# Attention over 128 half heads on one core: three planner constants, a planner that may mix two chains, K's second copy in two halves, fewer self-waits

## The chip, the cores and the metric

One core of a Trainium2 chip (trn2). The metric is the device time of one execution in microseconds (us), lower is better. Ratios are the mean time of one kernel's fast runs over the mean of the other's fast runs of the same rounds, so not quite the ratio of the medians that are quoted.

## The reference

```python
q (8, 8, 1024, 64), k and v (8, 2, 1024, 64), float32, values about 0.1
for each of 2 key/value heads, for its 4 query heads:
    scores = q @ k.T / 8
    attn = exp(scores - max);  attn /= attn.sum() + 1e-8
    out = attn @ v
```

The kernel leaves out the maximum (scores are small) and divides by the sum at the end; the sum comes from a column of ones beside v.

## The kernel before: the parts that matter

In the lines of the profile `aps` is a PSUM buffer with two scores for ScalarE, `dps` a bank with one score for VectorE, `ops` a bank of outputs (PSUM is the memory in which TensorE's results lie here, a bank one piece of it); `p_ring` and `pd` hold finished exponentials, `z` and `y` what a chain has in between, `kset` K.

There are 128 jobs (8 batches, 8 heads, even and odd query rows), each of 8 cells of 128 keys by 512 queries, 1024 cells in all. A cell needs a score matmul (`qk`) on TensorE, an exponential, and an output product (`pv`, four matmuls of 65 columns). Two roads lead through the exponential:

- road A, ScalarE: two cells at once (a *pair* of scores) in one of two PSUM buffers, one `exp` of 128x1024;
- road D, VectorE with GpSimd: a *conversion* (`p1`) of one cell into 16-bit integers, then for each ten cells a *chain* of four steps that corrects the bits: `and`, `line` (on GpSimd), `prod`, `add`.

`norm` is the normalisation of a finished job on VectorE (a reciprocal and a multiplication). Which cell takes which road, and in which order each engine works, is decided by a greedy planner in the kernel, which keeps a clock for every engine and always takes the operation that it believes can start first:

```python
QK, PV, P1, NORM = 0.216, 0.1225, 0.603, 0.555
EXP = (0.05, 0.4268)
FOUR, TWO, POOL_ONE = (0.20, 0.133), (0.16, 0.27), (0.25, 0.43)   # fixed, per cell: and / prod, add / line
... AHEAD = 0.04                                                  # lead of the scores for ScalarE
FIRST_TURN = 3.3                                                  # when the odd side's K is there
...
while normed < nj:
    ...                                        # road A: one more score of a pair
            best = min(best or (INF,), (t - AHEAD, 1, "qk", 0, t))
    ...                                        # road D: one more score for VectorE
            best = min(best or (INF,), (t, 2, "qk", 1, t))
    ...                                        # pv, norm, p1, and the first chain in the queue
```

The engines run the operations in this order, whatever time they really take. In an exp:

```python
if n >= P_TILES and n % OBSERVE == 0:          # P_TILES = 28 output tiles in a ring, OBSERVE = 8
    seen = exp_ins[n - P_TILES + OBSERVE - 1]
    tc.add_manual_dep(act.ins, seen.name, SYNC, reason="ring")      # self-wait: ScalarE for ScalarE
```

At the start, the even side's K lies in partitions 0 to 63 and is copied to partitions 64 to 127 for the odd side:

```python
nc.scalar.copy(out=qT[(0, 0)][:, : HALF // 2], in_=tq[0][:, : HALF // 2])
turn_k(1, slice(0, NHC), 0)
last_score[0] = keep_warm(4)
put_k(0, 1, slice(0, NHC), 0)
nc.gpsimd.dma_start(out=ksets[0][hi, 0, 1, :], in_=ksets[0][lo, 0, 0, :])
```

The softmax here doesn't subtract the row's maximum and nothing guards it: scores larger than these inputs give would overflow.

## Time and profile before

| | before |
|---|---|
| time | 386.97 us, median of 3 (386.77 to 387.01) |
| span of the traced execution | 384.92 us |
| exps, conversions | 406, 212 |
| end of the fourth exp | 10.82 us |
| distance between the ends of later exps | 0.917 us |
| last exp ends, then to the end | 379.33, 5.59 us |

The lines behind this table are in the prediction below. How to read it: ScalarE's exps form one row without holes from the fourth to the last, so the time is the start, plus the number of exps times 0.917 us, plus every lateness of an exp, plus what follows the last. I number exps from 0 ("the fourth" is number 3). *Late* means: the end of an exp lies more than 0.917 us behind the end of the one before; the surpluses of 5 ns or more are added up, good to about 0.01 us. In before, from the fifth exp on, they come to 0.01 us.

### The profile page before, as it was taken

How to read it: one execution, taken by the hardware profiler on the slowest of the kernel's cores; microseconds unless marked ns; L12 is line 12 of the kernel's file. 1: busy time of each engine (PE TensorE's matmuls, PEld its weight loads, DVE VectorE, ACT ScalarE, POOL GpSimd, SP SyncE). 2: the span in 40 equal slices, each digit the busy share in tenths (PEclk: the TensorE clock that was granted, in tenths of full speed). 3: DMA queues.
4: the chain of work that ended last, by engine and by line, in shares of the span. 5: the costliest groups of instructions: out<-in, count | busy, mean ns of one | idle time of the engine just before them, and what ended most of it. 6: DMA issues, size and time to landing. Idle time of an engine off the chain costs nothing.

```text
span 384.9 us, 12057 instructions
## 1 busy us (share of the span) xinstructions
PE 368.1 (96%) x5172; PEld 234.5 (61%) x5172; DVE 350.1 (91%) x544; ACT 375.1 (97%) x411; POOL 165.3 (43%) x147
## 2 busy tenths in 40 slices
PE   8879999999999999999999999999999999999985
PEld 6425565656666666666666565666566566666654
DVE  4879999999999999999999999999999999999692
ACT  5999999999999999999999999999999999999994
POOL 5394571716246171625535252535445261531410
PEclk9999999999999999999999999999999999999998
DMA  8888979597859769595865949486584756621213
GB/s 137 152 130 141 141 138 173 113 129 148 128 111 134 132 109 141 123 138 85 151 123 126 125 90 169 74 150 113 119 143 109 111 100 113 109 70 29 71 43 83
DMA packets 102422, 45.49 MB, mean 118 GB/s; under 512 B 63776, under 2 KB 100896, under 8 KB 101120
## 3 DMA queue, kind: packets, MB, share of 16 engines
q1 hardware_dynamic: 82096, 31.21, 37.5%
q0 software_dynamic: 19728, 13.25, 29.8%
q8 instruction: 40, 0.66, 0.8%
q10 hardware_dynamic: 544, 0.26, 0.2%
q14 instruction: 14, 0.11, 0.1%
HBM read 25.17 MB, written 27.00 MB: 136 GB/s over the span
## 4 chain that ended last, share of the span: by engine, by line
ACT 94%; PE 2%; DMA 1%; issue 1%; DVE 0%; SPq 0%; POOLq 0%
ACT p_ring L463 94%; PE ops L522 1%; PE aps L452 1%; DMA fk<-in_k_dram 1%; DMA kset<-kset 1%; SPq L389 0%; DVE ost L538 0%; ACT hk L411 0%; DVE kset L382 0%; DVE qT L427 0%; PE aps L373 0%; DVE rec L535 0%; PE ops L419 0%; PE ops L400 0%; POOLq L433 0%
## 5 line engine op out<-in xcount | busy, mean ns | idle before, releaser
L463 ACT ACTIVATE p_ring<-aps 128x1024 bf16<-128x1024 f32 x406 | 372.4, 1100 | 1.2 <-PE aps L452 1.2
L452 PE MATMUL aps<-qT,kset 128*128 128x512 bf16 x812 | 240.6, 378 | 11.4 <-ACT p_ring L463 8.8
L522 PEld LDWEIGHTS <-p_ring 128*128 128x128 bf16 x3248 | 137.5, 97 | 60.4 <-ACT p_ring L463 0.2
L522 PE MATMUL ops<-vset,p_ring 128*128 128x65 bf16 x3248 | 150.8, 194 | 0.1
L477 DVE TENSOR_SCALAR pd<-dps 128x512 uint16<-128x512 f32 x212 | 138.0, 682 | 13.2 <-PE dps L452 12.3
L500 POOL TENSOR_SCALAR y<-z 128x5120 f16<-128x5120 uint16 (+1 forms) x22 | 94.6, 4301 | 82.7 <-DVE rec L535 45.0
L452 PEld LDWEIGHTS <-kset 128*128 128x128 bf16 x1024 | 82.6, 97 | 58.8 <-issue 26.7
L314 POOL DMA_DIRECT2D scr_q<-in_q_dram x63 | 34.7, 551 | 99.0 <-PE aps L452 47.6
L452 PE MATMUL dps<-qT,kset 128*128 128x512 bf16 x212 | 73.4, 378 | 0.0
L511 DVE TENSOR_TENSOR pd<-pd,y 128x5120 uint16<-128x5120 uint16 (+1 forms) x22 | 59.8, 2719 | 0.1
L509 DVE TENSOR_TENSOR y<-z,y 128x5120 f16<-128x5120 uint16 (+1 forms) x22 | 59.8, 2718 | 0.0
L538 DVE TENSOR_TENSOR ost<-ops,rec 128x256 f32<-128x256 f32 x128 | 54.3, 424 | 4.4
L522 PEld LDWEIGHTS <-pd 128*128 128x128 bf16 x848 | 41.3, 98 | 25.6 <-DVE pd L511 3.6
L522 PE MATMUL ops<-vset,pd 128*128 128x65 bf16 x848 | 48.4, 194 | 0.0
L496 DVE TENSOR_SCALAR z<-pd 128x5120 uint16<-128x5120 uint16 (+1 forms) x22 | 31.7, 1443 | 0.6
L535 DVE RECIPROCAL rec<-ops 128x4 f32<-128x4 f32 x128 | 22.5, 176 | 9.8 <-PE ops L522 8.8
L347 POOL DMA_DIRECT2D vset<-in_v_dram x32 | 24.9, 782 | 0.0
L314 POOL DMA_DIRECT2D scr_k<-in_k_dram x15 | 7.8, 521 | 24.1 <-PE aps L452 16.7
L400 PE MATMUL ops<-blank 128*128 128x128 bf16 x40 | 4.4, 286 | 1.1 <-DVE blank L279 1.1
L400 PEld LDWEIGHTS <-blank 128*128 128x128 bf16 x40 | 3.8, 135 | 1.1 <-DVE blank L279 1.1
L354 POOL DMA_DIRECT2D kset<-kset x6 | 3.2, 537 | 0.0
L411 ACT ACT_TABLE_LOAD x1 | 1.3, 1283 | 1.8 <-issue 1.8
(23 smaller groups left out, 8.7 us busy)
## 6 DMA issues: line engine op xcount, KB each, us to landing
out_dram<-ost SPq DMA_DIRECT2D x63, 256.0 KB, 2.9
scr_q<-in_q_dram POOLq DMA_DIRECT2D x63, 128.0 KB, 3.6
kset<-kT SPq DMA_DIRECT2D x60, 64.0 KB, 3.1
vset<-in_v_dram POOLq DMA_DIRECT2D x32, 64.0 KB, 4.0
scr_k<-in_k_dram POOLq DMA_DIRECT2D x15, 128.0 KB, 3.2
qT<-scr_q SPq DMA_TRANSPOSE x63, 4.0
kset<-kset POOLq DMA_DIRECT2D x7, 128.0 KB, 4.0
fq<-in_q_dram ACTq DMA_DIRECT2D x2, 128.0 KB, 3.2
```

The lines of the kernel that those rows point to most:

```text
L314: dma = nc.gpsimd.dma_start(out=scr.rearrange("(p f) -> p f", f=1024), in_=src.rearrange("(p s) d -> p (s d)", s=1024 // D),)
L347: nc.gpsimd.dma_start(out=vsets[b % 2][:, g, two * NHC : (two + 1) * NHC, 0:D], in_=v[b, g].rearrange("(c p two) d -> two p c d", p=128, t ...
L452: last_score[0] = nc.tensor.matmul(dst, lhsT=ksets[b % 2][:, h // HPG, side, c * 128 : (c + 1) * 128], rhs=qT[(b, h)], start=True, stop=Tr ...
L463: act = nc.scalar.activation(out=pt[:, 0:m], in_=psum.pop(("A", n))[:, 0:m], func=AF.Exp, scale=scale)
L477: nc.vector.tensor_scalar(out=groups[g][:, slot], in0=psum.pop(cell), scalar1=bits_scale, scalar2=bits_bias, op0=ALU.mult, op1=ALU.add,)
L496: eng.tensor_scalar(out=z, in0=pd, scalar1=0x7F, scalar2=None, op0=ALU.bitwise_and)
L500: eng.tensor_scalar(out=y, in0=z, scalar1=CURVE_A / 128.0, scalar2=CURVE_B, op0=ALU.mult, op1=ALU.add,)
L509: eng.tensor_tensor(out=y, in0=z, in1=y, op=ALU.mult)
L511: eng.tensor_tensor(out=pd, in0=pd, in1=y, op=ALU.add)
L522: nc.tensor.matmul(ops_of[s][:, qs, :], lhsT=p_of[cell][:, qs * 128 : (qs + 1) * 128], rhs=vsets[b % 2][:, h // HPG, c, :], start=opens an ...
L535: nc.vector.reciprocal(out=rec, in_=o[:, :, D])
L538: nc.vector.tensor_tensor(out=stage[(b, h)][:, :, side, :], in0=o[:, :, 0:D], in1=rec.unsqueeze(2).to_broadcast([128, NQS, D]), op=ALU.mult,)
```

## The change

The intent: let the planner mix the steps of two chains, with a model of the SBUF port that VectorE and GpSimd share; give it smaller fixed costs of the chain's steps and no lead for ScalarE's scores; bring half of K's second copy earlier; drop most self-waits.

```diff
-    FOUR, TWO, POOL_ONE = (0.20, 0.133), (0.16, 0.27), (0.25, 0.43)
+    FOUR, TWO, POOL_ONE = (0.09, 0.133), (0.05, 0.27), (0.25, 0.43)
-    ... AHEAD, FIRST_PV = 28, 5, 16, 2, 6, 6, 0.04, 2.0
+    ... AHEAD, FIRST_PV = 28, 5, 16, 2, 6, 6, 0.0, 2.0
-    FIRST_TURN, FIRST_LOAD, EACH_LOAD = 3.3, 4.5, 4.2
+    FIRST_TURN, FIRST_LOAD, EACH_LOAD = 2.4, 4.5, 4.2
...
+        for i, (at, _, _, step) in enumerate(chainq):
+            if CHAIN[step] in ON_POOL:
+                at = max(at, pool, two_end)
+            else:
+                at = max(at, dve, pool)
+            best = min(best or (INF,), (at, 2 + i, "chain", i))
...
-    OBSERVE = 8
+    OBSERVE = 26
-        if n >= P_TILES and n % OBSERVE == 0:
+        if n >= P_TILES and (n - P_TILES) % OBSERVE == 0:
...
+        nc.scalar.dma_start(
+            out=ksets[0][hi, 0, 1, :HALF], in_=ksets[0][lo, 0, 0, :HALF]
+        )
         turn_k(1, slice(0, NHC), 0)
         last_score[0] = keep_warm(4)
         put_k(0, 1, slice(0, NHC), 0)
-        nc.gpsimd.dma_start(out=ksets[0][hi, 0, 1, :], in_=ksets[0][lo, 0, 0, :])
+        nc.gpsimd.dma_start(
+            out=ksets[0][hi, 0, 1, HALF:], in_=ksets[0][lo, 0, 0, HALF:]
+        )
```

Cut: two constants that switch nothing on (their values are 0), the bookkeeping of the two new clocks (`pool`, `two_end`), and a test for empty chain parts.

## The prediction

> **What bounds the kernel now.** I read the page first (busy shares, chain by line, groups), then the waits, then the chain in order of time at the start and at the end, then the timelines of ScalarE and TensorE in those stretches.
>
> ```profile
> PE 368.1 (96%) x5172; PEld 234.5 (61%) x5172; DVE 350.1 (91%) x544; ACT 375.1 (97%) x411; POOL 165.3 (43%) x147
> ...
> ACT 94%; PE 2%; DMA 1%; issue 1%; DVE 0%; SPq 0%; POOLq 0%
> ...
> L463 ACT ACTIVATE p_ring<-aps 128x1024 bf16<-128x1024 f32 x406 | 372.4, 1100 | 1.2 <-PE aps L452 1.2
> L477 DVE TENSOR_SCALAR pd<-dps 128x512 uint16<-128x512 f32 x212 | 138.0, 682 | 13.2 <-PE dps L452 12.3
> ```
>
> ScalarE's exps are the path: 406 of them, 372.4 us busy, that is 0.917 us each although one lasts 1100 ns (neighbours overlap), and only 1.2 us of idle before them in the whole run. The other score cells (212 of 1024; an exp covers two cells) go through VectorE: one conversion each (L477), and for every ten cells a chain of four steps, and and prod and add on VectorE, line on GpSimd. VectorE's 13.2 us of idle before conversions is its slack.
>
> The chain in order of time, then the timelines of ScalarE and of TensorE at the start, show where the path is not ScalarE:
>
> ```profile
> 6.63 2.48 DMA kset<-kset
> 9.15 0.62 PE aps L452 x2
> ```
> ```profile
> 6.47 2.85 ACT L463 ACTIVATE p_ring<-aps 128x1024 bf16<-128x1024 f32 x3 [0.68 <-PE aps L452]
> 9.80 23.94 ACT L463 ACTIVATE p_ring<-aps 128x1024 bf16<-128x1024 f32 x26 [0.47 <-PE aps L452]
> ```
> ```profile
> 9.15 1.04 PE L452 MATMUL aps<-qT,kset 128*128 128x512 bf16 x4 [0.27 <-DMA kset<-kset]
> ```
>
> Columns of a timeline row: start, duration, then the work. Three exps run from 6.47, ending at 9.32; the fourth starts at 9.80, because its scores wait for the second copy of K (SBUF to SBUF, issued by GpSimd at 6.63, landed at 9.11). A free-standing exp takes 1.02 us from start to end, a following one ends 0.917 after the last, so the fourth ends at 10.82 where 10.24 was possible: the wait costs 0.58 us.
>
> The end, from the chain in order of time:
>
> ```profile
> 366.34 6.59 ACT p_ring L463 x7
> 372.92 0.04 issue
> 372.96 0.59 PE aps L452 x2
> ...
> 377.62 0.52 PE aps L452 x2
> 378.14 2.60 PE ops L522 x84
> ```
>
> The last exp ends at 379.33 in the timeline, but TensorE works until 380.74: after the last score it still has 84 output matmuls, 21 cells of 4, back to back (2.60 / 21 = 0.124 us a cell). So the last 1.4 us, and the normalisation behind it (0.66) and the store, follow a TensorE backlog, not the exp.
>
> **What the Trainium skill says.** "ScalarE: Activation LUTs", section "What ACT_TABLE_LOAD costs": with immediate scale and bias an ACTIVATE takes 186 ns + 0.833 ns per element, and back-to-back ones overlap by about 93 ns. For 1024 elements that is 1039 ns alone and 946 ns in a row; the trace has 1020 and 917. The measured figures decide; both say that the period is ScalarE's own, not a wait for scores. "SBUF — State Buffer", section "Who interferes with whom": a VectorE instruction with two SBUF inputs, or in a 2-port mode, and a GpSimd instruction that reads SBUF hold the shared port by turns, the later one blocks fully. The trace of before cannot test it: no and, prod or add lies beside a line, and the full lines take 4.45 to 4.48 us whatever conversions and normalisations lie beside. "DMA: Bandwidth & Descriptors", section "Latency and other measured facts": first byte about 0.6 us from a hardware-generated queue (ScalarE's, SyncE's) and 1 us from GpSimd's. I use only the direction; the GpSimd copy at hand took 2.48 us from issue to landing, ScalarE's two loads from HBM 3.1 and 3.4.
>
> **The change part by part.** The kernel's order comes from a planner inside it, so I compared the built programs' instruction orders.
>
> 1. *The new model.* Despite the intent no two chains mix: in both orders each and, line, prod, add is over before the next chain's and. What changes is the split. After has 404 exps and 216 conversions (before 406 and 212): the lower fixed costs of the chain steps let VectorE take four cells more, and the last chain has six cells, not two. On the path: 2 exps less x 0.917 = **-1.83 us**.
>  Can VectorE carry it? After places a chain about every 18 exps, 18 x 0.917 = 16.5 us. From the distances between ends in the trace, for ten cells: 10 conversions x 0.60 + 5.75 normalisations x 0.55 (0.09 + 0.46) + and 1.45 + prod 2.73 + add 2.73 = 16.1 us. It fits with 0.4 us to spare, 97% busy; before had a chain every 17 us or so. What is lost: prod now stands straight behind the earliest end of line, where before about 0.5 us lay between, so each late GpSimd start (before: 3 of 22 lines started 0.4 to 1.1 us after their and, behind DMA issues) now holds VectorE, and may hold TensorE at a conversion bank. I put **+0.2 us** on it, a guess from three such starts of which half is absorbed.
>
> 2. *Lead of score matmuls from 0.04 to 0.* TensorE may now put an output or a VectorE score in front of an exp's scores. The exps were fed with only 0.47 us of idle after the start, and each such swap is at most one score matmul, 0.216 us; most is hidden by the second PSUM buffer. **0**.
>
> 3. *K's second copy.* Its even half leaves on ScalarE's queue, where it waits only for a VectorE copy done at 4.76 and ScalarE's own copy done at 5.52, so issue at about 5.6, and not at 6.63 behind the odd half (L382 ends at 6.02). With the 2.5 to 3.1 us seen from issue to landing it lands at 8.1 to 8.7. The fourth exp's scores are free to run only when the second exp's PSUM buffer is (ends 8.40, so about 8.55), behind one more score for VectorE: at landing up to 8.35 nothing of the 0.58 us remains, at 8.7 some 0.35. The issue takes about 0.5 us of ScalarE's queue (its earlier two: 0.48 and 0.53), to 6.1, before the first exp at 6.47. The odd half is still on GpSimd, needed only from the fifth exp. **-0.45 us**, of 0.58 at most.
>
> 4. *Self-waits.* 51 exps carry a wait for an earlier exp before, 15 after. The chain shows an "issue" of about 0.04 us at each; were that real, 36 x 0.045 = 1.6 us would come back. But the 26 exps from 9.80 to 33.74 hold one such wait and run at (23.94 - 1.02) / 25 = 0.917; the 360 from 36.37 to 366.34, each eighth with one, at 329.97 / 360 = 0.917. A waiting exp starts later and ends when it would have: **0**.
>
> 5. *The end.* In the new order 13 cells of output follow the last score, not 21: 8 x 0.124 = 1.0 us less backlog. But the last exp then bounds too: it ends about 1.19 us after the last score (379.33 - 378.14), and two cells follow, 0.16 + 0.25, so 1.6 us, the same as 13 x 0.124. From 2.60 to 1.6: **-1.0 us**. In before TensorE stood idle for about 0.33 us before each of three score pairs from 369 on, with the outputs waiting for the last full chain; in after's order these outputs come earlier.
>
> Sum: -1.83 + 0.2 - 0.45 - 1.0 = -3.1 us, from 386.97 to **383.9 us** (0.992).
>
> **The rivals.**
> - *VectorE becomes the bound.* For it: 97% by my sum, and prod without slack behind line. If each of some 20 chains held up the exps by 0.15 us, +3 us: 386.9, no gain. Against: before's VectorE was idle about 21 us between 12 and 372 us by its gaps, and the additional work is 4 x 0.6 + 4 cells of chain (0.13 + 0.27 + 0.27) = 5 us.
> - *The self-waits do cost what the chain shows.* Then 1.6 us more, 382.3. Against it: point 4.
> - *The copy on ScalarE's queue delays the first exp,* or lands no sooner than GpSimd's. Then 0 to +0.4 instead of -0.45: about 384.5. For it: ScalarE's earlier DMAs took longer to land than GpSimd's copy, though from HBM.
> - *The tail's order does not hold on the chip*: the outputs of the last six-cell chain are late and the backlog stays 2.6 us: 384.9.
>
> **Range and chances.** Sure are the two exps; the others make the range: 382.7 if the self-waits pay in part and the start gains all of its 0.58, 385.8 if VectorE's stalls take 2 us. Executions of one kernel spread by 0.1% here. Faster by over 2% needs 379.2, 4.7 us beyond the sum, and no wait of that size is left; slower by over 2% needs 7.7 us of new ScalarE idle in a plan of the same kind. Chances 0.01, 0.97, 0.02.
>
> **What would show each step.** 404 exps at 0.917 each, with under 1 us of idle in total (step 1 and 2; idle before exps in the middle of the run, released by scores, means VectorE bounds). VectorE's idle before conversions falls from 13 us to under 9, and a row of waits of VectorE for line appears. The fourth exp starts at 9.2 to 9.4, the first at 6.47 as before (step 3); a first exp after 6.6 refutes it. Exps without self-wait at 0.917 confirm step 4, at 0.90 refute it. The last output run of the chain is x52, about 1.6 us, and the exp or TensorE end together (step 5). The prediction fails if exps show idle in the middle of the run, or if their period changes.

## The result, and the profile after

385.77 us, median of 4 (385.70 to 385.81), against 386.99 of before; ratio 0.9968, interval 0.9951 to 0.9986. The gain is 1.2 us where 3.1 were predicted; the time lies at the upper end of the predicted range (385.8).

From the page of the changed kernel: busy shares, the chain by engine, and two groups (after the bar: busy us, mean ns of one; then idle before, and what ended it).

```profile
PE 365.6 (95%) x5172; PEld 233.6 (61%) x5172; DVE 353.8 (92%) x548; ACT 374.6 (98%) x409; POOL 174.4 (45%) x147
...
ACT 86%; PE 10%; DVE 2%; issue 1%
...
L477 ACT ACTIVATE p_ring<-aps 128x1024 bf16<-128x1024 f32 x404 | 371.8, 1067 | 1.4 <-PE aps L466 1.2
L491 DVE TENSOR_SCALAR pd<-dps 128x512 uint16<-128x512 f32 x216 | 138.6, 683 | 7.0 <-PE dps L466 6.7
```

404 exps and 216 conversions, as read from the order. The idle time before exps is 1.4 us, no more than the 1.2 of before, so by the idle column the exps are fed as well as ever. That column misleads here. Two exps overlap by up to 0.18 us on ScalarE, so one that comes up to that much late leaves no hole. Its lateness shows in two other places of the same line: busy divided by count is 371.8 / 404 = 0.9203 (before 372.4 / 406 = 0.9172), and the mean of one fell from 1100 to 1067 ns, because a late exp spends less time overlapped with its forerunner. 404 x 0.0031 = 1.25 us is most of what is missing. The chain says it too: 10% of it now runs through TensorE, where it was 2%.

The start. First four transposes and the first scores on TensorE's timeline, before, then after:

```profile
5.18 0.39 PE L373 MATMUL dps<-ident,hk 128*128 128x128 bf16 x4
5.84 1.02 PE L452 MATMUL aps<-qT,kset 128*128 128x512 bf16 x4
```
```profile
5.73 0.63 PE L382 MATMUL dps<-ident,hk 128*128 128x128 bf16 x4
```
```profile
5.94 0.56 ACTq L439 DMA_DIRECT2D kset<-kset  x1
7.40 23.94 ACT L477 ACTIVATE p_ring<-aps 128x1024 bf16<-128x1024 f32 x26 [1.23 <-PE aps L466]
```

The same four transposes took 0.63 instead of 0.39 us (314 against 219 ns each): TensorE was still at its slow clock. The record of the granted clock begins at full speed at 6.96 us in this execution, at 4.08 in the trace of before. In all thirteen traces the first exp follows that moment: it starts at 6.41 to 6.47 where the clock was full by 4.3, and later with each later clock, up to 7.40 at 6.96. So the first exp starts at 7.40, not 6.47, and then 26 exps run in one piece; the hole before the fourth is gone. The fourth ends at 11.18, later than the 10.82 of before.

The end, from the chain in order of time:

```profile
377.86 0.43 PE aps L466 x2
378.29 1.64 PE ops L538 x52
```

52 output matmuls follow the last score, not 84, in 1.64 us, not 2.60: as predicted.

The middle. From exp 127 to exp 325, once in each chain of 18 exps, one exp comes about 0.05 us late (12 times), with some 0.013 on the one or two ahead of it; elsewhere a few come 0.07 to 0.21 late (numbers 27, 28, 34, 72, 89, 381, 393). Here is one regular case, exp 145, which starts at 141.02. TensorE's timeline, then VectorE's:

```profile
137.93 0.41 PE L538 MATMUL ops<-vset,p_ring 128*128 128x65 bf16 x8
138.29 0.38 PE L466 MATMUL dps<-qT,kset 128*128 128x512 bf16 x1
138.51 0.59 PE L466 MATMUL aps<-qT,kset 128*128 128x512 bf16 x2
138.94 0.38 PE L466 MATMUL dps<-qT,kset 128*128 128x512 bf16 x1
139.40 0.59 PE L466 MATMUL aps<-qT,kset 128*128 128x512 bf16 x2
...
140.17 0.38 PE L466 MATMUL dps<-qT,kset 128*128 128x512 bf16 x1
140.38 0.59 PE L466 MATMUL aps<-qT,kset 128*128 128x512 bf16 x2
```
```profile
135.59 1.50 DVE L512 TENSOR_SCALAR z<-pd 128x5120 uint16<-128x5120 uint16 x1
137.00 0.18 DVE L551 RECIPROCAL rec<-ops 128x4 f32<-128x4 f32 x1
137.22 0.42 DVE L554 TENSOR_TENSOR ost<-ops,rec 128x256 f32<-128x256 f32 x1
137.56 2.49 DVE L491 TENSOR_SCALAR pd<-dps 128x512 uint16<-128x512 f32 x4
```

Matmuls are pipelined: a score takes 0.216 us from start to start, a cell of outputs 0.123. Two cells of outputs from 137.93 end at 138.17; the score for VectorE (dps) follows only at 138.29. It waited 0.12 us for a bank: VectorE was in its `and` (z, 1.5 us), then a normalisation, and its first conversion (137.56 + 0.68) freed a bank at 138.24. From there TensorE works without a gap, and in front of the pair for exp 145 (aps at 140.38) stands one more score for VectorE (140.17). Two successive pairs begin at 139.40 and 140.38, 0.98 us apart where ScalarE needs one each 0.917. So both the rival "VectorE" and step 2 of the prediction may have a share; the experiments part them. The regular stalls and the small ones ahead of them are about 0.7 us of the 1.6; the other 0.9 are the irregular ones.

The sum, from the ends of the exps in the traces (the control is e1 below, the changed kernel a second time):

| us against before | predicted | after's trace | control's trace |
|---|---|---|---|
| two exps less | -1.83 | -1.83 | -1.83 |
| to the end of the fourth exp | -0.45 | +0.36 | -0.47 |
| late exps from the fifth on | +0.2 | +1.60 | +2.05 |
| after the last exp | -1.0 | -1.00 | -1.01 |
| sum, and the span's difference | -3.1 | -0.87, -0.89 | -1.26, -1.30 |

Of the control's 2.05, 0.47 is the fifth exp and belongs to the start; from the sixth exp on it is 1.59, as in after.

### The profile page after: what moved, and what is told of

It is laid out like the page before. It is cut to its first block, busy times and chain, and to the rows that moved or that the text cites. A ratio compares the mean times of both kernels' runs of the same rounds, so it can differ in the third digit from the quotient of the medians.

```text
span 384.0 us, 12026 instructions
## 1 busy us (share of the span) xinstructions
PE 365.6 (95%) x5172; PEld 233.6 (61%) x5172; DVE 353.8 (92%) x548; ACT 374.6 (98%) x409; POOL 174.4 (45%) x147
## 4 chain that ended last, share of the span: by engine, by line
ACT 86%; PE 10%; DVE 2%; issue 1%
ACT p_ring L477 86%; PE aps L466 4%; PE ops L538 4%; PE ops L409 1%; PE dps L466 1%; DVE pd L527 1%; DVE ost L554 0%; DVE y L525 0%; DVE z L512 0%; DVE rec L551 0%; PE dps L382 0%; PE dps L428 0%; PE ops L428 0%; PE aps L382 0%; DVE blank L288 0%
## 5 line engine op out<-in xcount | busy, mean ns | idle before, releaser
L477 ACT ACTIVATE p_ring<-aps 128x1024 bf16<-128x1024 f32 x404 | 371.8, 1067 | 1.4 <-PE aps L466 1.2
L538 PEld LDWEIGHTS <-p_ring 128*128 128x128 bf16 x3232 | 140.1, 98 | 64.0
L538 PE MATMUL ops<-vset,p_ring 128*128 128x65 bf16 x3232 | 154.6, 194 | 0.0
L516 POOL TENSOR_SCALAR y<-z 128x5120 f16<-128x5120 uint16 (+1 forms) x22 | 96.4, 4383 | 70.0 <-DVE rec L551 48.7
L466 PEld LDWEIGHTS <-kset 128*128 128x128 bf16 x1024 | 79.7, 97 | 56.4 <-issue 25.8
L323 POOL DMA_DIRECT2D scr_q<-in_q_dram x63 | 39.1, 621 | 83.5 <-PE dps L466 44.3
L466 PE MATMUL dps<-qT,kset 128*128 128x512 bf16 x216 | 76.4, 379 | 0.0
L525 DVE TENSOR_TENSOR y<-z,y 128x5120 f16<-128x5120 uint16 (+1 forms) x22 | 61.0, 2772 | 1.1 <-POOL y L516 1.1
L538 PEld LDWEIGHTS <-pd 128*128 128x128 bf16 x864 | 42.8, 98 | 24.7 <-DVE ost L554 2.2
L538 PE MATMUL ops<-vset,pd 128*128 128x65 bf16 x864 | 52.2, 194 | 0.3
L323 POOL DMA_DIRECT2D scr_k<-in_k_dram x15 | 9.8, 656 | 39.9 <-PE aps L466 33.0
```

Of the source, the lines that this page charges most:

```text
L323: dma = nc.gpsimd.dma_start(out=scr.rearrange("(p f) -> p f", f=1024), in_=src.rearrange("(p s) d -> p (s d)", s=1024 // D),)
L466: last_score[0] = nc.tensor.matmul(dst, lhsT=ksets[b % 2][:, h // HPG, side, c * 128 : (c + 1) * 128], rhs=qT[(b, h)], start=True, stop=Tr ...
L477: act = nc.scalar.activation(out=pt[:, 0:m], in_=psum.pop(("A", n))[:, 0:m], func=AF.Exp, scale=scale)
L516: eng.tensor_scalar(out=y, in0=z, scalar1=CURVE_A / 128.0, scalar2=CURVE_B, op0=ALU.mult, op1=ALU.add,)
L525: eng.tensor_tensor(out=y, in0=z, in1=y, op=ALU.mult)
L538: nc.tensor.matmul(ops_of[s][:, qs, :], lhsT=p_of[cell][:, qs * 128 : (qs + 1) * 128], rhs=vsets[b % 2][:, h // HPG, c, :], start=opens an ...
```

## The experiments

| run | exps | median us (range) | ratio to before | 95% interval | clock full at | 4th exp ends | late from the 5th on |
|---|---|---|---|---|---|---|---|
| before | 406 | 386.97 (386.77-387.01) | | | 4.08 | 10.82 | 0.01 |
| after | 404 | 385.77 (385.70-385.81) | 0.9968 | 0.9951-0.9986 | 6.96 | 11.18 | 1.62 |
| e1_again | 404 | 385.62 (385.39-385.71) | 0.9965 | 0.9952-0.9977 | 3.90 | 10.35 | 2.06 |
| e2_pairs_first | 404 | 385.31 (384.88-385.70) | 0.9958 | 0.9945-0.9970 | 5.73 | 11.06 | 1.24 |
| e3_convert_first | 404 | 385.19 (384.44-385.38) | 0.9951 | 0.9939-0.9964 | 4.73 | 10.32 | 1.13 |
| e4_k_vector | 404 | 385.10 (384.97-385.63) | 0.9954 | 0.9941-0.9968 | 5.31 | 10.60 | 1.60 |
| e5_k_whole | 404 | 385.87 (385.75-386.37) | 0.9976 | 0.9963-0.9988 | 6.10 | 11.72 | 1.59 |
| e6_waits8 | 404 | 386.13 (385.58-386.41) | 0.9981 | 0.9968-0.9995 | 5.04 | 10.71 | 1.94 |
| e7_split_only | 406 | 386.62 (386.26-387.18) | 0.9989 | 0.9976-1.0001 | 4.30 | 10.43 | 0.01 |
| e8_lead | 407 | 387.79 (387.60-388.21) | 1.0019 | 1.0006-1.0031 | 6.27 | 10.84 | 0.87 |
| e9_first_and_k | 404 | 384.49 (384.26-385.06) | 0.9941 | 0.9928-0.9953 | 6.61 | 11.00 | 1.02 |
| e10_sizes | 403 | 384.00 (383.62-384.58) | 0.9925 | 0.9913-0.9938 | 4.73 | 10.46 | 1.56 |
| e11_blank_later | 403 | 383.44 (383.19-383.72) | 0.9904 | 0.9889-0.9920 | 6.38 | 11.03 | 0.89 |

The last three columns are of the one traced execution, the times of all (4 or 5; before 9 in each batch, medians 386.97 to 387.12). All results were correct. The runs came in three batches (e1 to e4; e5, e6, e9, e10; e7, e8, e11), before's own medians differ by 0.15 us between them, so medians across batches are good to some 0.2 us; the first batch also ran on another chip than the other two. By the 2% mark every run counts as the same as before; what is said below rests on ranges, intervals and traces.

**A comparison without a run.** The kernel before, with nothing of the new planner code but its three constants (and the new self-waits and the split copy), builds to the same instructions and waits in the same order on every engine as the changed kernel. So at these constants the mixing of chains and the port model, the headline of the change, alter nothing. Nor do the constants act one by one. Counted from the order that before's planner gives: lower chain costs alone 406 exps, no lead alone 409, K's earlier time alone 407; costs and lead together 404, all three 404.

**e1_again: the changed kernel once more.** No edit.

> The changed kernel once more, unchanged, as a control for the start. In its first trace TensorE's granted clock rose to full at 6.96 us, in the trace of before at 4.08, and the first exp started at 7.40 against 6.47. Theory (the second copy of K bounds the start, so the clock is hidden): 385.7 to 385.9 us whatever the moment of the clock; the fourth exp ends at 11.0 to 11.2 us. Rival (the clock's moment is the cause of the late start and falls by chance): executions spread by up to 0.9 us, and a trace with an early clock has the fourth exp ending near 10.3 us.

385.62 us. The clock came at 3.90, and the fourth exp ended at 10.35, as the rival had it. But the time hardly moved. ScalarE's timeline, and the chain in order of time:

```profile
6.41 3.94 ACT L477 ACTIVATE p_ring<-aps 128x1024 bf16<-128x1024 f32 x4 [0.68 <-PE aps L466]
10.71 21.19 ACT L477 ACTIVATE p_ring<-aps 128x1024 bf16<-128x1024 f32 x23 [0.37 <-PE aps L466]
```
```profile
6.25 3.77 DMA kset<-kset
10.03 0.05 issue
10.07 0.62 PE aps L466 x2
```

Now four exps run in one piece and the fifth is 0.47 us late: its scores wait for K's other half, which GpSimd issued at 6.25 and which took 3.77 us to land. In this trace the wait has moved from the fourth exp to the fifth, and of 0.99 us between the two first exps only 0.35 is left at the fifth (11.74 against 12.09). But that is not the rule. In the five other traces of the changed start (after, e2, e3, e6, e8) the other half landed 2.2 to 2.7 us after its issue and the fifth exp was on time; in e3, with the clock at 4.73, it ended at 11.24, 0.85 before after's. Why the transfer took 3.77 us here is not shown. Both ideas were right in part: chance moves the clock, and the landing of a half, which varies too, hides more or less of it.

**e2_pairs_first: order on TensorE only.** At 17 places the VectorE score goes behind the pair.

```diff
-    plan = make_plan(len(jobs), NKC)
+    plan = pairs_first(make_plan(len(jobs), NKC))
```

> At 17 places where an exp came late in the trace, the VectorE score right in front of the exp's two scores goes behind them; nothing else moves. Theory (the planner's lead of 0 lets VectorE scores in front, and these exps wait for that): most of the stalls of these 17 exps and of the exps just ahead of them goes, about 1.1 us in all: 384.7 us; the periods of exps 127, 145, 163 fall from 0.965 to 0.917. Rival (VectorE is the bound, the order on TensorE only shows where): the stalls stay or move to the next exps, 385.6 to 386.2 us.

385.31 us, between the two. Eleven of the twelve regular stalls are gone, so the score in front of the pair is a necessary part. The twelfth, kept with 0.036 at exp 288, was not in the list of moves: exp 289 has the score in front, but 288 carries a self-wait and takes over most of its lateness (in e6, with no self-wait at 288, exp 289 is 0.047 late instead). But exp 36 is now 0.21 us late where exp 34 had been 0.12, and exps 74, 85, 91, 109 are late in place of 72, 83, 89, 107. Where TensorE has no gap to give, moving a score moves the stall: 0.35 us less in sum than the control from the sixth exp on (1.24 against 1.59), not 1.1. Two small stalls are new, 0.04 and 0.03 us at exps 184 and 236; both carry a self-wait (see e6).

**e3_convert_first: order on VectorE only.** After each `and` the first conversion goes ahead of the normalisation (19 places).

```diff
-    plan = make_plan(len(jobs), NKC)
+    plan = convert_first(make_plan(len(jobs), NKC))
```

> After each and the first conversion goes in front of the normalisation, so that a bank for VectorE scores is free 0.55 us sooner; TensorE's order is untouched. Theory (each regular stall needs both: TensorE waits 0.12 us for a bank that VectorE frees late behind and and a normalisation, and has no gap afterwards to catch up before the exp): the wait for the bank once a chain goes, and with it the 12 regular stalls of 0.05 us and the small ones ahead of them, 0.7 us: 385.1 us. Rival (order on TensorE alone): 385.7 us, stalls as before. Second rival: the normalisation 0.6 us later holds up the next output bank, over 386 us.

385.19 us, as the theory had it; in the trace the lateness from the sixth exp on fell by 0.46 (1.13 against 1.59), not by 0.7. VectorE's timeline, then TensorE's, at the same place:

```profile
134.81 1.49 DVE L524 TENSOR_SCALAR z<-pd 128x5120 uint16<-128x5120 uint16 x1
136.22 0.68 DVE L503 TENSOR_SCALAR pd<-dps 128x512 uint16<-128x512 f32 x1
136.82 0.17 DVE L563 RECIPROCAL rec<-ops 128x4 f32<-128x4 f32 x1
```
```profile
137.14 0.41 PE L550 MATMUL ops<-vset,p_ring 128*128 128x65 bf16 x8
137.38 0.38 PE L478 MATMUL dps<-qT,kset 128*128 128x512 bf16 x1
...
139.33 0.38 PE L478 MATMUL dps<-qT,kset 128*128 128x512 bf16 x1
139.55 0.59 PE L478 MATMUL aps<-qT,kset 128*128 128x512 bf16 x2
```

The VectorE score now follows the outputs at once (137.14 + 0.246 = 137.38). One still stands in front of the pair at 139.55, and the exp is on time: exps 127 to 325 are 0.013 late at most. Each regular stall needs both, a late bank and the score in front; taking away either ends it. Exp 89 got worse (0.27 for 0.15), which took back 0.12.

**e4_k_vector: the even half of K by VectorE.** The transposed tile holds the even half in partitions 64 to 127 as well, so no transfer is needed.

```diff
-        nc.scalar.dma_start(
-            out=ksets[0][hi, 0, 1, :HALF], in_=ksets[0][lo, 0, 0, :HALF]
-        )
...
         put_k(0, 1, slice(0, NHC), 0)
+        put_k(1, 0, slice(0, NHC), 0)
```

> The even half of K's second copy comes from the transposed tile by one VectorE copy of 64x512 (0.42 us as its neighbour), ready at about 6.5 to 7.4 us, in place of the transfer over ScalarE's queue that landed at 9.02; the rest as after. Theory (the landing of that half bounds the start when TensorE's clock rises early; when late, the clock does): with an early clock the fourth exp ends at 10.2 to 10.4 and the time is 384.8 to 385.0; with a late clock 385.7; executions spread between the two. Rival (the start is bound by the other half, by GpSimd, or the start does not matter): 385.7 to 385.9 in all executions.

385.10 us, with executions from 384.97 to 385.63, of the spread that the theory asked for. The clock came at 5.31, the first exp at 6.83, and the fourth exp ended at 10.60, 3.77 after: no hole. Against the control 0.5 us by the medians, and four of the five executions are faster than the control's fastest.

**e5_k_whole: the split undone.**

```diff
-        nc.scalar.dma_start(
-            out=ksets[0][hi, 0, 1, :HALF], in_=ksets[0][lo, 0, 0, :HALF]
-        )
...
-        nc.gpsimd.dma_start(
-            out=ksets[0][hi, 0, 1, HALF:], in_=ksets[0][lo, 0, 0, HALF:]
-        )
+        nc.gpsimd.dma_start(out=ksets[0][hi, 0, 1, :], in_=ksets[0][lo, 0, 0, :])
```

> The changed kernel with K's second copy in one piece on GpSimd again, as in before; the order of all else is after's. Theory (the two half copies land no sooner than the whole one did, the start is bound by a landing near 9 to 10 us or by a late clock): 385.5 to 385.9 us, the fifth exp ends within 0.3 us of the control's 11.74 (early clock) or 12.09 (late clock). Rival (the split brings its 0.45 us): 386.0 to 386.2.

385.87 us, inside the theory's range, but 0.25 above the control of the other batch, and no execution as fast as the control's slowest. The fourth exp ended at 11.72 and the fifth 0.917 later, at 12.64, outside the 0.3 us expected: with the clock at 6.10 the copy's source was ready late, GpSimd issued it at 7.36 and it landed at 9.79. So the split is worth about 0.25 us here, not 0.45; the intervals overlap, and it is not sure.

**e6_waits8: the self-waits back.**

```diff
-    OBSERVE = 26
+    OBSERVE = 8
```

> The changed kernel with a self-wait every 8 exps again, 50 or so in place of 15. Theory (a waiting exp starts later and ends when it would have): no change, 385.5 to 385.8 us. Rival (0.045 us each, as the chain's issue pieces have it): 35 x 0.045 = 1.6 us more, 387.2.

386.13 us, between the two: 0.5 above the control, but that is of another batch, and the intervals of the two ratios overlap. The self-waiting exps are numbers 28, 36, 44 and so on. Every exp that is late here and was not in the control is one of them: 36, 68, 260, 276 and 396 anew (0.007 to 0.21 us), while 180, 252 and 324 take over the lateness of the exp behind them and add next to nothing. From the sixth exp on the lateness is 1.94 us, 0.35 over the control's 1.59. In before the self-waits cost next to nothing (0.013 at exp 184), since every exp had its scores in time. My reading, not shown apart from this: a self-wait takes away the early start that lets an exp absorb scores that come late, so it costs where the feed is tight. The large one, exp 276, has matmul records missing next to it, and I cannot say why it is 0.21; without it 0.14 us is left in this one trace.

**e7_split_only: the split in the kernel before.** Edit: as in the change, at the same place.

> The kernel before with K's second copy split as in the change and nothing else. Theory (the half lands at 8.4 to 9.0 us, and two of the fourth exp's scores follow at once): the 0.58 us before the fourth exp shrinks by 0.2 to 0.5, 386.5 to 386.8 us. Rival (the halves land no sooner): 387.0.

386.62 us, ratio 0.9989, interval up to 1.0001: about 0.4, the sign not certain. The trace agrees with the theory: the fourth exp ended at 10.43, 0.39 sooner, the half landing at 8.72.

**e8_lead: the lead back to 0.04.**

```diff
-    ... AHEAD, FIRST_PV = 28, 5, 16, 2, 6, 6, 0.0, 2.0
+    ... AHEAD, FIRST_PV = 28, 5, 16, 2, 6, 6, 0.04, 2.0
```

> The changed kernel with the planner's lead of score matmuls at 0.04 again: its order has 407 exps and 14 output cells behind the last score. Theory (lead 0 bought three exps less, 2.75 us, with stalls of 1.6): stalls under 0.4 us after the fifth exp, 386.7 to 387.2 us. Rival (the stalls are VectorE's and come in any order with these costs): stalls of 1.2 us and more, over 387.6.

387.79 us, slower than before: above the theory's range and within the rival's, but by other terms than the rival's. From the traces against the control: three exps more +2.75, fifth exp later +0.02 (the fourth is 0.49 later, with the clock at 6.27 for 3.90, but the control then loses 0.47), late exps from the sixth on -0.72, tail +0.13, in sum +2.18; the spans differ by 2.21. The stalls did fall (0.87, of which 0.48 at exps 26 to 28), but not below the 0.4 expected. So lead 0, which I had called worth nothing, decides the sign of the whole change: with it the order has three exps less, and pays with 0.7 us of stalls. That it does so by letting VectorE's scores go first is argued from the planner, not shown.

**e9_first_and_k: e3 (but for the fifth chain, ahead of exp 89) and e4 together.**

```diff
-    plan = make_plan(len(jobs), NKC)
+    plan = convert_first(make_plan(len(jobs), NKC))     # not for the fifth chain
+        put_k(1, 0, slice(0, NHC), 0)                   # for ScalarE's transfer, as in e4
```

> Conversion ahead of the normalisation after each and (but for the chain where that gave exp 89 a longer stall), and the even half of K by a VectorE copy: the two parts that gained alone. Theory (they are independent, 0.5 us of stalls and 0.4 of start): 384.5 us, 384.2 to 384.9 with the clock; stalls after the fifth exp about 1.0 us. Rival (the start's gain is lost to the next wait): 385.1, as each alone.

384.49 us, as the theory had it, with 1.02 us of lateness left: the two gains add up, as far as medians of two batches can be compared.

**e10_sizes: other constants.** Found by trying some thousand settings and stepping through the order that each gives with the durations of the traces, to see where TensorE has too much work between two pairs.

```diff
-    QK, PV, P1, NORM = 0.216, 0.1225, 0.603, 0.555
+    QK, PV, P1, NORM = 0.216, 0.1225, 0.598, 0.555
-    FOUR, TWO, POOL_ONE = (0.09, 0.133), (0.05, 0.27), (0.25, 0.43)
+    FOUR, TWO, POOL_ONE = (0.12, 0.133), (0.03, 0.27), (0.25, 0.43)
-    FIRST_TURN, FIRST_LOAD, EACH_LOAD = 2.4, 4.5, 4.2
+    FIRST_TURN, FIRST_LOAD, EACH_LOAD = 3.3, 4.5, 4.2
+        put_k(1, 0, slice(0, NHC), 0)                   # as in e4
```

> The planner with four other sizes (0.12 and 0.03 for the fixed costs of the chain's steps, 0.598 for a conversion, 3.3 for the second side's start), and the even half of K by a VectorE copy: 403 exps, and by a count over the order few places where TensorE has more than 0.917 us of work between two pairs and no gap before. Theory (what the change lost, it lost to stalls that the order makes, so an order with as few exps and few of them gets the 1.5 us back): stalls under 0.5 us after the fifth exp, 383.7 to 384.3 us. Rival (at 403 exps VectorE is at its limit whatever the order): stalls of over 1.5 us, 384.8 or more.

384.00 us, inside the theory's time, but with 1.56 us of lateness, not 0.5, so the time was right for other reasons than the theory's: in the traces against the control one exp less brought 0.92, a shorter tail 0.45 and the start 0.37 (to the fifth exp), and the stalls from the sixth on were the same. They are of another kind: 0.95 of it are two exps near the start, number 26 (0.64) and number 6 (0.31), which the count did not see. Exp 26, VectorE, then GpSimd:

```profile
16.05 1.49 DVE L510 TENSOR_SCALAR z<-pd 128x5120 uint16<-128x5120 uint16 x1
...
23.20 2.83 DVE L523 TENSOR_TENSOR y<-z,y 128x5120 f16<-128x5120 uint16 x1 [2.00 <-POOL y L514]
```
```profile
16.28 1.36 POOL L323 DMA_DIRECT2D scr_q<-in_q_dram  x1 [1.45 <-PE aps L464]
17.63 1.04 POOL L363 DMA_DIRECT2D kset<-kset  x2
18.69 4.48 POOL L514 TENSOR_SCALAR y<-z 128x5120 f16<-128x5120 uint16 x1
```

The `and` ended at 17.54, but GpSimd had a load and two zero copies to issue first and began `line` at 18.69; `prod` waited 2.0 us for it. The load's issue took 1.36 us and ended 0.10 after the `and`; such an issue takes 0.51 alone. The last section counts this hold over a whole trace.

**e11_blank_later: four zero copies later.**

```diff
-            at(9.0 + 2.0 * n, blank_k, s, g, side)
+            at(9.0 if n == 0 else 19.0 + 2.0 * n, blank_k, s, g, side)
```

> e10_sizes with GpSimd's four copies of zeros for the second K buffer issued some 12 us later, behind the first chain's line. In e10's trace exp 26 came 0.64 us late: GpSimd began the first line 1.15 us after its and, behind such copies, VectorE's prod waited 2.0 us for it, and TensorE's outputs for the add. Theory: that stall goes, 383.3 to 383.5 us. Rival (exp 26 is late by the order): as e10, 384.0.

383.44 us, as the theory had it. (In the traces the two pairs of copies moved from 17.63 and 23.65 to 26.31 and 29.26, so by 8.7 and 5.6 us, not by 12.) VectorE's timeline:

```profile
22.75 2.83 DVE L523 TENSOR_TENSOR y<-z,y 128x5120 f16<-128x5120 uint16 x1 [0.98 <-POOL y L514]
```

The wait for `line` halved and exp 26 is on time; exp 6 is still 0.31 late. This version is faster than both kernels: 0.9904 of before (interval 0.9889 to 0.9920), and 2.2 us under the control's median of another batch.

## Why the prediction was wrong, point by point

- *What bounds the kernel*: right. ScalarE's row of exps, 0.917 us each when on time, in every run.
- *Two exps less, -1.83*: right in number, and so was the remark that no two chains mix. The identical build makes it stronger: port model and mixing do nothing at these constants. The reason given, that "the lower fixed costs of the chain steps let VectorE take four cells more", was wrong: with these costs and the old lead e8 has 407 exps. It takes the lead as well, which step 2 called worth nothing.
- *VectorE can carry it at 97% busy, +0.2*, and *lead 0: each swap is hidden, 0*: these two steps failed; together they measured +1.6 us. I weighed VectorE's work of a whole chain (16.1 of 16.5 us) and the largest single swap (0.216 us) apart from each other. What counted in the regular stalls was a short stretch: after `and` and a normalisation a bank comes 0.12 us late, TensorE has no gap in the next two pairs to catch up, and then the swapped score does not fit. e2 and e3 show that each half alone is harmless; that accounts for the 0.7 us of the regular stalls (e3 leaves 0.1 of them). The other 0.9 also came as scores that were late, but why is partly open (last point). I also looked for stalls as idle time before exps, where they cannot be seen while they are shorter than the overlap. And I had used before's well-fed exps as proof that a swap is absorbed, though before has the lead: in e8 it takes away 0.72 of the 1.59 us.
- *Where VectorE's limit would show*: I expected waits for `line`. Two came, at 59.6 and 343.8 us, 1.1 us in sum; the regular stalls came from `and`, which had been given 1.42 us in the planner (0.09 + 10 x 0.133) and takes 1.49; whether these 0.07 us are what makes the bank late was not tested.
- *K's second copy, -0.45*: failed in its parts. In after the half was issued at 5.94 and landed at 9.02, after 3.08 us, at the end of the assumed 2.5 to 3.1, and later than the 8.7 allowed. The fourth exp's wait went, but the first exp came at 7.40, past the 6.6 that was to refute the step, through TensorE's clock, which I did not foresee, and not through ScalarE's queue. In the control the clock was early, the half went at 5.49 and landed at 8.42, and the fourth exp gained 0.47 as predicted; then the other half, called needed "only from the fifth exp", stopped the fifth for as long. Over the six traces of this start the fifth exp ended between 0.50 us sooner and 0.36 later than in before. The direction that I took for the two queues' DMAs ("I use only the direction") does not show from issue to landing: in the seven traces with the split, halves on ScalarE's queue took 2.7 to 3.2 us, on GpSimd's 2.2 to 2.8 (3.77 once). By e5 the split is worth some 0.25 us in the new order, by e7 about 0.4 in the old, unsure.
- *Self-waits, 0*: right for before's order (0.01 us in all), not in general: in e6's trace they cost 0.35 us in the changed order, 0.21 of it at one exp, so that they cost something is likely and how much is open.
- *The end, -1.0*: right in size and in its line (x52, 1.64 us).
- *The shared port, "the trace of before cannot test it"*: it could, at GpSimd's DMA issues. Five of the seven beside an `and` in before ended 94 to 99 ns after it and took 0.63 to 1.41 us, where 0.51 is usual.
- *Open*: the single 0.21 us at exp 276 in e6; the stalls at 27, 34 and 393, ahead of which TensorE waits for VectorE (for a normalisation that frees an output bank, it seems, at 27 and 393, for a conversion bank at 34), and which no run took away in the changed order (e2 only moved the one at 34 to 36); and exp 6 in e10 and e11.

## What to carry to other kernels

When instructions of the bounding engine overlap, look for lateness in busy time divided by count and in the mean duration, not in the idle column; the feed can lose 1.6 us of 385 with the idle time unchanged. In a greedy plan the constants choose among whole orders: a lead of 0.04 us moved three exps, and only together with the smaller costs, which alone moved none; and the named idea of a change may not act at all, which comparing the built orders tells without a run. Check slack in the tightest stretch, across two engines at once, not as an average over a period.

## What the Trainium skill lacked or had wrong

- "TensorE: Matmul & The Clock Gate", "Part 1: The HAM clock gate (the "warmup" mystery)": it has what I missed. It says that the activity window of 3413 ns runs freely, so that the moment of full speed varies. The traces agree: full speed came between 3.90 and 6.96 us in thirteen executions of near identical starts, and the granted-full stretches were 378.88 or 375.47 us long, 3.41 apart. Its "±500ns" is too narrow here, where it was 3.1 us from the first to the last.
- "SBUF — State Buffer", "A bandwidth-pool intuition that's wrong (but worth ruling out)": it says that a GpSimd DMA issue that meets a VectorE operation holding the shared port is blocked to that operation's end plus about 115 ns. In after's trace the twelve issues that began during an `and` (one of them 0.01 us before it) ended 93 to 103 ns after it and took 1.31 us in the mean, 0.51 away from any chain step. It agrees, with a slightly smaller tail. Loads that began beside `prod` or `add` took 0.51, as alone.
- "ScalarE: Activation LUTs", "What ACT_TABLE_LOAD costs": about 93 ns of overlap gives 946 ns for 1024 elements in a row; measured 917 (and 1020 alone, for 1039). The passage does not say where its tile lay; the exps here read PSUM.
- No page that I read says that an overlapped ScalarE slice hides a late feed: mean 1100 to 1067 ns while idle went from 1.2 to 1.4 us.
- No page that I read gives the price of a wait of an engine for itself: 0.01 us over 51 exps that were fed in time, 0.35 in sum over 47 where some were fed late (one trace, 0.21 of it at one exp).
